# A decoder layer in f32 on one core: GLA score products paired with a later turn, head gates behind the next head's keys and queries, branch outputs stored whole, and another order of the first loads

## The chip, the cores and the metric

The kernel runs on one core of one Trainium2 chip. The metric is device time in microseconds (us) of one execution, taken as the median of several runs.

## The reference

One layer of a hybrid trunk is computed in f32 on 16 meta tokens and 1024 tokens of width 1024. An RMS norm is followed by one wide projection `h @ w_in + b_in`, whose columns are the inputs of four GLA heads, four mLSTM heads and two merge gates. A GLA head is gated linear attention with a decay per channel:

```
diff = bc[t] - bc[s]                       # running sums of log decay, per channel
scores[t, s] = sum_k q[t, k] * k[s, k] * exp(diff[t, s, k])     for s <= t
out = inter + scores @ v
o_gla = head_rms(out) * silu(g_r)
```

The mLSTM heads are a matrix memory behind a short convolution. Both branches are normed per head, multiplied by their head gate, projected, merged as `sigmoid(gate_a) * (o_gla @ w_bg) + sigmoid(gate_b) * (o_ml @ w_bm)`, projected again and added to the input. A convolutional gated MLP and a last norm follow.

## The kernel before, in words

Every large product is made of three: each operand is split into a high part H and a rest L (types that TensorE streams at one pass), and H·H, H·L and L·H are added in PSUM. The split of a loaded weight is `prep` (L96): a DMA on SyncE's queue into one of two `wr` buffers, an ACT copy that makes `wH_...`, a DVE subtraction that makes `wL_...`. The units are loaded in the order in which `head_units` and `gate_units` name them.

The stages are these.

1. Start (L323 to L344). Nine token tiles `xt` (the first holds the 16 meta tokens) are loaded; `norm_x` squares and sums a tile on ACT (`xj`), takes the root on GpSimd (`xr`), scales on DVE, transposes eight blocks on TensorE into PSUM (`xtp`, L316), and splits the result into `xH` (ACT, L318) and `xL` (DVE, L320), which stay in SBUF as the moving operands of all projections.
2. Heads (L861 to L874). `main` walks the projections: `proj_cm` (L146) makes 24 products for each third of the tokens (`TH_ALL`, `TH_POST`: 342 to 348 columns; for head 0 quarters, `SEG_ALL`, `SEG_POST`), `proj_v` (L172) 24 products of 256 columns for each token tile. After each such group `advance` takes one step of the head that was projected before (`gla`, `mlstm`; each `yield` is a step), so that TensorE has a long group between two short steps. Before the change the order for head s is: gate of s (`gate_proj`, the rows `r`), keys and queries of s+1, values of s+1, merge gate a.
3. A GLA head (L551). The scores of each 128 token chunk are built level by level: `level(b)` (L610) scales keys of the early half and queries of the late half of each block of 2b tokens against the block's middle, on DVE (L624, L625, L628), ACT (L626) and GpSimd (L627). For b = 1, 2, 4, 8, 16 `scores_later` (L580) makes one f32 product per chunk, 128 rows by the 64 late columns, and copies what lies in the blocks by a mask into `A` (L589). For b = 32 and 64 `scores_pair` (L567) makes four products of 128 columns, each for two chunks. The diagonal comes first (L564, copied by mask in L565). The running state, the outputs `op` (L720, L721) and their squares follow; `post` (L510) scales each chunk by its norm (L520), transposes it on TensorE (`ot`, L530), multiplies by the gate (L532), splits it into `oH` and the rest (L540, L541) and stores both. `of` and `oH` have one buffer each.
4. Behind head 0 stands `small_rows` (L450), the scalar gates of all four mLSTM heads: two scans and some 1040 element rows on DVE, activations with other tables on ACT.
5. Merge (L917 to L960). `load_o` (L884) loads the H and L parts of eight output tiles for each branch; `bg` and `bm` are the branch products (L909). Then come the output product (L1193), the FFN up (L1107) and the FFN down (L1323), which the change doesn't touch.

The instruction order of each engine comes from a scheduler, which works on the program's order with the priorities that `hp` sets.

Of the kernel before, what the change touches and what calls it, by code (L numbers as in the profile page):

```python
# [1 line left out]

# [6 lines left out]
F32 = mybir.dt.float32  # L9
F32R = mybir.dt.float32r  # L10
U8 = mybir.dt.uint8
# [33 lines left out]
def hybrid_kernel(ctx, tc, x, meta, norm_mix, w_in, b_in, gla_w_gate, gla_b_gate, gla_norm,  # L45
# [60 lines left out]
    lrHL = [wp.tile([P, NK, P], F32R, name=f"w{p}_lr", tag="w" + p) for p in "HL"]  # L106
    for t in lrHL:
        nc.vector.memset(t.bitcast(F32), 0.0)
# [104 lines left out]
    def head_units(s):  # L213
        h = s % 4
        if s < 4:
            uk[s], uq[s] = u_cm(w_in, O_GK + P * h, f"gk{h}"), u_cm(w_in, O_GQ + P * h, f"gq{h}")
            if s == 0:
                uk["lr"] = U.add()
            uv[s] = u_v(O_GV + DV * h, f"gv{h}_")
        else:  # L220
            uk[s], uq[s] = u_cm(w_in, O_MK + P * h, f"mk{h}"), u_cm(w_in, O_MQ + P * h, f"mq{h}")
            uv[s] = u_v(O_MV + DV * h, f"mv{h}_")

    def gate_units(s):
        h = s % 4
        o = (O_GR if s < 4 else O_MO) + DV * h
        ur[s] = [u_cm(w_in, o + P * j, f"r{s}_{j}") for j in range(2)]

    head_units(0)
    for s in range(8):  # L230
        gate_units(s)
# [25 lines left out]
    va = hd.tile([P, T], F32, name="va", tag="oH", bufs=1)[:, :P]  # L257
# [31 lines left out]
    xts = []  # L289

    def load_x(*tiles):
        for i in tiles:
            n = NM if i == 0 else P
            tag, bufs = [("w", 5), ("q", 2), ("k", 2)][(i >= 5) + (i >= 7)]
            xt = hd.tile([P, T], F32, name=f"xt{i}", tag=tag, bufs=bufs)
# [3 lines left out]
    def norm_x(i):  # L299
# [4 lines left out]
        junk = hd.tile([P, T], F32, name=f"xj{i}", tag="of", bufs=1)  # L304
# [7 lines left out]
        for g in range(2):  # L312
            tp = ps.tile([P, 4, P], F32, name=f"xtp{i}_{g}", tag="s", bufs=3)
# [3 lines left out]
            h4 = xH[:, 4 * g:4 * g + 4, c0:c0 + n]  # L317
            nc.scalar.activation(h4, tp[:, :, :n], AF.Copy)  # L318
            l4 = xL[:, 4 * g:4 * g + 4, c0:c0 + n]
            nc.vector.tensor_tensor(l4, tp[:, :, :n], h4.bitcast(F32), OP.subtract)  # L320
# [11 lines left out]
    load_x(4, 5)  # L332
    U.get(2, 0)
    norm_x(3)
    load_x(6, 7, 8)
    for dst, ap in small:
        nc.sync.dma_start(dst, ap)
    for i in range(4, NC + 1):
        if i == NC:
            columns()  # L340
        last = norm_x(i)
    for t, c in ((xH, 0), (xL, 32)):
        m3 = xM[:, :48 * NK].rearrange("p (k w) -> p k w", w=48)
        nc.scalar.activation(m3[:, :, c:c + NM], t[:, :, :NM].bitcast(F32), AF.Copy)  # L344
    floor[0] = tc.cur_priority
# [8 lines left out]

    def cc(i):
        return col[:, i:i + 1]


    with tc.issue_after(last.ins):
        lmask = {}  # L360
        mfs = hd.tile([P, T], F32, name="mfs", tag="raw", bufs=1)
        for i, b in enumerate((16, 8, 4, 2, 1)):
            mf = mfs[:, 64 * i:64 * (i + 1)]
            half = mf.rearrange("p (n w) -> p n w", w=b)
            nc.gpsimd.memset(half, 1.0)
            nb = P // (2 * b)
            nc.gpsimd.affine_select(out=half, in_=half, compare_op=OP.is_ge, fill=0.0, base=0,
                                    pattern=[[-2 * b, nb], [0, b]], channel_multiplier=1)
            nc.gpsimd.affine_select(out=half, in_=half, compare_op=OP.is_ge, fill=0.0, base=b - 1,
                                    pattern=[[2 * b, nb], [0, b]], channel_multiplier=-1)  # L370
            mu = hd.tile([P, 64], U8, name=f"mu{b}")
            nc.vector.tensor_copy(mu, mf)
            lmask[b] = mu
        mu = hd.tile([P, P], U8, name="mu0")
        nc.vector.tensor_copy(mu, ident)
        lmask[0] = mu
        big = hd.tile([P, P], F32, name="big")
# [5 lines left out]
    osc = {(g, p): dram.tile([NK, P, NP], F32, name=f"osc{g}{p}") for g in "gm" for p in "HL"}  # L383
# [5 lines left out]
    def head_proj(s):  # L389
# [7 lines left out]
        if s < 4:  # L397
# [4 lines left out]
            if s == 0:  # L402
                yield from together(pk, pq, proj_cm(uk["lr"], SEG_ALL, 0, lambda p, t0, n: nc.scalar.activation(
                    raw_s[0:96, t0:t0 + n], p[0:96, :], AF.Identity, bias=bsm[0:96])))
# [14 lines left out]
    def gate_proj(s):  # L419
        hh = heads[s]  # L420
        hh["r"] = []
        for j in range(2):
# [3 lines left out]
            yield from proj_cm(ur[s][j], TH_POST, T0, lambda p, t0, n, r=r, c=c: nc.scalar.activation(  # L426
# [83 lines left out]
    def post(s, o, om, sc, ncols, last):  # L510
# [13 lines left out]
        for j in range(2):  # L524
            r = hh["r"][j]
            of = hd.tile([P, T], F32, name=f"of{s}_{j}", tag="of", bufs=1)
# [12 lines left out]
            oH = hd.tile([P, NP], F32R, name=f"oH{s}_{j}", tag="oH", bufs=1)  # L539
            nc.scalar.activation(oH, of[:, :NP], AF.Copy)  # L540
            nc.vector.tensor_tensor(of[:, :NP], of[:, :NP], oH.bitcast(F32), OP.subtract)  # L541
            nc.sync.dma_start(osc[g, "H"][2 * h + j], oH.bitcast(F32))
            nc.sync.dma_start(osc[g, "L"][2 * h + j], of[:, :NP])
# [7 lines left out]
    def gla(s):  # L551
# [7 lines left out]
        def scores(lt, rt, b):  # L559
            for g in range(2):  # L560
                pt = ps.tile([P, 4, P], F32, name=f"sc{s}_{b}_{g}", tag="s", bufs=3)
                for i in range(4):
                    c = 4 * g + i
# [872 lines left out]
```

## Time and profile before

| | us |
|---|---|
| median of 3 runs | 1971.62 (1969.85 to 1973.77) |
| the profiled execution | 1973.3 |
| its span, first to last instruction | 1971.4 |
| TensorE busy, matmuls / weight loads | 1936.3 / 1854.0 |
| DVE / ACT / GpSimd busy | 963.4 / 744.3 / 286.5 |

In the profile PE is TensorE's matmul row, PEld its weight loads, POOL is GpSimd, SP the queue that issues DMAs. A matmul of two f32 operands stands in the trace as two records (320 records in L586 for the 160 products of the program), a product of split operands as one. A matmul's recorded time reaches past the start of the next one, so that slots are read from start to start. PEclk is the clock granted to TensorE, 1.00 being full. An idle time stands at the instruction that ended it, with what released it.

### The profile page before, as it was taken

Reading aid. Unit: us, or ns where it says so; the run is one execution under the profiler, and the core shown is the slowest. Engines: PE = TensorE matmul, PEld = TensorE weight load, DVE = VectorE, ACT = ScalarE, POOL = GpSimd, SP = SyncE. Lnnn points to the kernel's source line nnn. Section 1 sums busy time; section 2 is a strip of 40 time slices with the busy share of each in tenths; the row PEclk is TensorE's granted clock in tenths of the full one; section 3 lists DMA queues with packets and bytes.
Section 4 is the critical chain, followed back from the end, with each engine's and each line's share of the span. In section 5 each row is a group of like instructions: output and inputs, shape, how many; then the busy total and the mean of one; then the engine's idle time right before and its main releaser. Section 6 shows DMA issues by size and latency. Waiting matters only on the chain. (4 is left out here: it accounts for less than half of the span.)

```text
span 1971.4 us, 31346 instructions
## 1 busy us (share of the span) xinstructions
PE 1936.3 (98%) x13333; PEld 1854.0 (94%) x13333; DVE 963.4 (49%) x1427; ACT 744.3 (38%) x1176; POOL 286.5 (15%) x201
## 2 busy tenths in 40 slices
PE   7999999999999999999999999999999999999998
PEld 6999999999999999999999999999999999978886
DVE  6265263637535343422022446698888888710202
ACT  5145333535534343423221234544545444431211
POOL 2020020101000000000000002012222222364220
PEclk9999999999999999999999999999999999999999
DMA  4210403232234222226971433333333333487731
GB/s 152 57 33 23 100 22 95 37 70 69 61 96 90 64 88 63 79 62 123 315 268 54 150 108 108 124 102 126 116 119 123 118 118 113 170 301 263 239 101 43
DMA packets 191271, 224.82 MB, mean 114 GB/s; under 512 B 11102, under 2 KB 150640, under 8 KB 191131
## 3 DMA queue, kind: packets, MB, share of 16 engines
q1 hardware_dynamic: 190843, 221.76, 37.2%
q8 instruction: 105, 1.72, 0.4%
q10 hardware_dynamic: 288, 1.05, 0.1%
q14 instruction: 35, 0.29, 0.0%
HBM read 166.07 MB, written 56.71 MB: 113 GB/s over the span
## 5 line engine op out<-in xcount | busy, mean ns | idle before, releaser
L1323 PE MATMUL pd<-ringH,a 128*128 128x512 f32 x416 | 131.6, 393 | 1.5 <-DMA a<-adrL 1.5
L154 PE MATMUL pj<-xH,wH_r 128*128 128x342 f32 x384 | 124.2, 323 | 0.4 <-ACT r L426 0.4
L154 PE MATMUL pj<-xH,wL_r 128*128 128x342 f32 x384 | 122.9, 320 | 0.0
L154 PE MATMUL pj<-xL,wH_r 128*128 128x342 f32 x384 | 122.5, 319 | 0.0
L1357 DVE TENSOR_TENSOR acc<-pd,acc 128x512 f32<-128x512 f32 x16 | 11.1, 692 | 196.3 <-PE pd L1323 196.3
L1323 PEld LDWEIGHTS pd<-ringH,a 128*128 128x128 f32 x416 | 78.0, 188 | 19.6 <-DMA a<-adrL 2.0
L1323 PE MATMUL pd<-ringL,a 128*128 128x512 f32 x208 | 82.5, 397 | 1.5 <-POOL ringL L1302 1.5
L197 PE MATMUL pv<-wH_gv,xH 128*128 128x256 f32 x256 | 75.4, 294 | 0.0
L197 PE MATMUL pv<-wH_mv,xH 128*128 128x256 f32 x256 | 74.2, 290 | 0.0
L1193 PE MATMUL po<-wL_wo,yH 128*128 128x256 f32 x256 | 72.0, 282 | 2.0 <-DVE wL_wo L103 2.0
L1193 PE MATMUL po<-wH_wo,yH 128*128 128x256 f32 x256 | 72.8, 284 | 0.9 <-DVE h L1200 0.9
L154 PEld LDWEIGHTS pj<-xH,wH_r 128*128 128x128 f32 x384 | 72.2, 188 | 1.1 <-ACT r L426 0.5
L627 POOL TENSOR_TENSOR pk<-pk,kT 128x512 f32<-128x512 f32 x24 | 40.2, 1685 | 226.9 <-ACT pk L626 226.8
L197 PE MATMUL pv<-wL_gv,xH 128*128 128x256 f32 x256 | 72.7, 284 | 0.0
L197 PE MATMUL pv<-wH_gv,xL 128*128 128x256 f32 x256 | 72.6, 283 | 0.0
L154 PEld LDWEIGHTS pj<-xL,wH_r 128*128 128x128 f32 x384 | 72.2, 188 | 0.0
L154 PEld LDWEIGHTS pj<-xH,wL_r 128*128 128x128 f32 x384 | 72.2, 188 | 0.0
L197 PE MATMUL pv<-wL_mv,xH 128*128 128x256 f32 x256 | 71.9, 281 | 0.0
L197 PE MATMUL pv<-wH_mv,xL 128*128 128x256 f32 x256 | 71.9, 281 | 0.0
L1193 PE MATMUL po<-wH_wo,yL 128*128 128x256 f32 x256 | 71.8, 281 | 0.0
L1154 DVE SCALAR_TENSOR_TENSOR cv<-u,fc,cv 128x1024 f32<-128x1024 f32 x44 | 69.4, 1578 | 0.4
L201 DVE TENSOR_TENSOR v<-pv,bB 128x256 f32<-128x256 f32 x64 | 27.0, 421 | 78.1 <-PE pv L197 77.9
(618 smaller groups left out, 6714.5 us busy)
## 6 DMA issues: line engine op xcount, KB each, us to landing
rd<-in_ffn_w_down_dram SPq DMA_DIRECT2D x36, 512.0 KB, 5.9
rg<-in_ffn_w_up_dram SPq DMA_DIRECT2D x22, 512.0 KB, 4.2
ru<-in_ffn_w_up_dram SPq DMA_DIRECT2D x22, 512.0 KB, 3.8
a<-adrH SPq DMA_DIRECT2D x44, 256.0 KB, 5.0
a<-adrL SPq DMA_DIRECT2D x44, 256.0 KB, 4.7
adrH<-aH SPq DMA_DIRECT2D x21, 512.0 KB, 2.6
adrL<-aL SPq DMA_DIRECT2D x21, 512.0 KB, 2.6
wr_r<-in_w_in_dram SPq DMA_DIRECT2D x16, 512.0 KB, 4.0
```

The source lines that it names most:

```text
L154: nc.tensor.matmul(pt[:, :n], a[:, k, :], b[:, k, base + t0:base + t0 + n], start=(i == 0), stop=(i == 3 * NK - 1))
L197: nc.tensor.matmul(pt[:, :DV], a[:, k, t0:t0 + P], b[:, k % 4, :], start=(i == 0), stop=(i == 3 * NK - 1))
L201: nc.vector.tensor_tensor(vt[:n, c, :DV], pt[:n, :DV], bB[:n, :], OP.add)
L627: nc.gpsimd.tensor_tensor(pe, pe, lv(kv, b)[:, :, 0, :], OP.mult)
L1154: nc.vector.scalar_tensor_tensor(y, u[:, j:SEQ + j], fc[:, j, jj:jj + 1], y, OP.mult, OP.add)
L1193: nc.tensor.matmul(pt[:, :DV], a, b[:, k % 4, :], start=(k == 0 and i == 0), stop=(k == NK - 1 and i == len(terms) - 1))
L1323: nc.tensor.matmul(pts[t][n], a[:, c], b[:, 512 * n:512 * n + 512], start=start and i == 0, stop=stop and i == 2)
L1357: nc.vector.tensor_tensor(acc[:, h], pts[t][n], acc[:, h], OP.add)
```

## The change

In the GLA heads the five small levels are laid out as the large ones were: of a pair of chunks the early halves of the even one stand as they are, those of the odd one from back to front, so that four products of 128 columns hold eight chunks (`scores_small`). The odd chunks' scores are then the wrong way round in time, and one f32 product with a matrix of ones on the other diagonal (`flip`), 128x512, turns them (`turn`); ACT copies the result into a tile of its own, `An`. The diagonal and the level b = 32 follow the turn. The early half's subtraction on DVE and multiplication (or copy) on GpSimd become two instructions, one of them writing from back to front.

For heads 0 to 5 the next head's keys and queries stand ahead of this head's gate. Head 0's first gate tile is projected with its keys and queries, in quarters; the small columns `lr` come behind, in thirds. `small_rows` moves from head 0 to head 3. `post` stores one whole f32 tile instead of two parts; `load_o` loads it and splits it on ACT and DVE. `of` has two buffers. At the top stand eight products of the identity with itself, the first token tile's load comes ahead of `gmix`, keys' and queries' weights ahead of the third token tile, and four small rows are issued from ACT's queue.

```diff
-    lrHL = [wp.tile([P, NK, P], F32R, name=f"w{p}_lr", tag="w" + p) for p in "HL"]
+    lr2 = hd.tile([P, 2, NK, P], F32R, name="w_lr", tag="v", bufs=2)
...
+    GATE_LATER = [s < 6 for s in range(8)]
...
     for s in range(8):
+        if GATE_LATER[s]:
+            kq_units(s + 1)
         gate_units(s)
...
-            tp = ps.tile([P, 4, P], F32, name=f"xtp{i}_{g}", tag="s", bufs=3)
+            tp = ps.tile([P, 4, P], F32, name=f"xtp{i}_{g}", tag="pj" if i == 1 else "s", bufs=3)
...
-    load_x(0)
-    nc.sync.dma_start(gmix, rowb(norm_mix, 0, D))
-    load_x(1, 2)
-    norm_x(0)
-    norm_x(1)
-    U.get(0, 0)
-    load_x(3)
-    U.get(1, 0)
-    norm_x(2)
...
+    def idle_products(n, name):
+        pt = ps.tile([P, P], F32, name=f"idle{name}", tag="ot", bufs=2)
+        for _ in range(n):
+            nc.tensor.matmul(pt, ident, ident, start=True, stop=True)
+    idle_products(8, "a")
+    for dst, ap in small[:4]:
+        nc.scalar.dma_start(dst, ap)
+    load_x(0, 1)
+    nc.sync.dma_start(gmix, rowb(norm_mix, 0, D))
+    load_x(2)
+    norm_x(0)
+    norm_x(1)
+    U.get(0, 0)
+    U.get(1, 0)
+    norm_x(2)
+    load_x(3)
...
-                yield from together(pk, pq, proj_cm(uk["lr"], SEG_ALL, 0, lambda p, t0, n: nc.scalar.activation(
+                yield from together(pk, pq, gate_proj(0, (0,)))
+                yield from proj_cm(uk["lr"], TH_ALL, 0, lambda p, t0, n: nc.scalar.activation(
...
-            oH = hd.tile([P, NP], F32R, name=f"oH{s}_{j}", tag="oH", bufs=1)
-            nc.scalar.activation(oH, of[:, :NP], AF.Copy)
-            nc.vector.tensor_tensor(of[:, :NP], of[:, :NP], oH.bitcast(F32), OP.subtract)
-            nc.sync.dma_start(osc[g, "H"][2 * h + j], oH.bitcast(F32))
-            nc.sync.dma_start(osc[g, "L"][2 * h + j], of[:, :NP])
+            nc.sync.dma_start(osc[g][2 * h + j], of[:, :NP])
...
+        An = hd.tile([P, T], F32, name=f"An{s}", tag="of", bufs=2)[:, :512].rearrange("p (i t) -> p i t", t=P)
+        Ac = [An[:, c // 2, :] if c % 2 else A[:, c, :] for c in range(NC)]
...
+        def turn():
+            pt = ps.tile([P, 4, P], F32, name=f"sct{s}", tag="s", bufs=3)
+            nc.tensor.matmul(pt, flip, A.rearrange("p (i c) t -> p i c t", c=2)[:, :, 1, :], start=True, stop=True)
+            nc.scalar.activation(An, pt, AF.Copy)
+        def products(pk, b):
+            pt = ps.tile([P, 4, P], F32, name=f"sc{s}_{b}", tag="s", bufs=3)
+            for i in range(4):
+                nc.tensor.matmul(pt[:, i, :], pk[:, P * i:P * (i + 1)], pk[:, 512 + P * i:512 + P * (i + 1)], start=True, stop=True)
+            return pt
...
-        def scores_later(pk, b):
-            n = P // (2 * b)
-            pt = ps.tile([P, NC, 64], F32, name=f"sc{s}_{b}", tag="s", bufs=3)
-            for c in range(NC):
-                l = lv(pk[:, P * c:P * (c + 1)], b)[:, :, 1, :]
-                nc.tensor.matmul(pt[:, c, :], pk[:, P * c:P * (c + 1)], l, start=True, stop=True)
-            dst = A.rearrange("p c (n h w) -> p c n h w", h=2, w=b)[:, :, :, 1, :]
...
+        def scores_small(pk, b):
+            pt = products(pk, b)
+            dst = A.rearrange("p (i c) (n h w) -> p i (c n) h w", c=2, h=2, w=b)[:, :, :, 1, :]
...
+            if b < 32:
+                e = pk[:, :512].rearrange("p (i n h w) -> p i n h w", n=64 // b, h=2, w=b)
+                pe = [e[:, :, :, 0, :], e[:, :, ::-1, 1, ::-1]]
...
-                nc.vector.tensor_tensor(pe, ref, b4[:, :, 0, :], OP.subtract)
+                for e, _, t in early:
+                    nc.vector.tensor_tensor(e, t[..., b - 1:b].to_broadcast(t.shape), t, OP.subtract)
...
-                nc.gpsimd.tensor_tensor(pe, pe, lv(kv, b)[:, :, 0, :], OP.mult)
+                for e, k, _ in early:
+                    nc.gpsimd.tensor_tensor(e, e, k, OP.mult)
...
             if b == 64:
-                scores_pair(pk, 32)
+                yield
+                turn()
+                yield
+                scores_diagonal()
+                scores_large(pk, 32)
...
-        if s == 0:
+        if s == 3:
             side.append(small_rows())
-        main(gate_proj(s))
-        if s < 7:
-            main(head_proj(s + 1))
+        nxt = head_proj(s + 1) if s < 7 else iter(())
+        if GATE_LATER[s]:
+            main(islice(nxt, 6))
+        main(gate_proj(s, (0, 1) if s else (1,)))
+        main(nxt)
...
-            for p in "HL":
-                nc.sync.dma_start(t[p, k // 4][:, k % 4, :NP].bitcast(F32), osc[g, p][k])
+            h, l = (t[p, k // 4][:, k % 4, :NP] for p in "HL")
+            nc.sync.dma_start(l.bitcast(F32), osc[g][k])
+            nc.scalar.activation(h, l.bitcast(F32), AF.Copy)
+            nc.vector.tensor_tensor(l, l.bitcast(F32), h.bitcast(F32), OP.subtract)
```

What moves on the engines is shown at three places. The first is TensorE's queue in head 0's levels; `sc_b` is the product of level b, `sc_0` the diagonal, `sct` the turn, and between two of these rows stand one or two groups of a projection. Before:

```order
L564 MATMUL sc_0_0_1021<-qT_415,kT_414 128x128 x4
L564 MATMUL sc_0_1_1027<-qT_415,kT_414 128x128 x4
...
L586 MATMUL sc_1_1171<-pk_1_1102 128x64 x8
...
L586 MATMUL sc_2_1213<-pk_2_1165 128x64 x8
...
L586 MATMUL sc_4_1265<-pk_4_1207 128x64 x8
...
L572 MATMUL sc_32_1397<-pk_32_1343 128x128 x4
```

The same place after the change:

```order
L616 MATMUL sc_1_1238<-pk_1_1167 128x128 x4
...
L616 MATMUL sc_2_1278<-pk_2_1230 128x128 x4
...
L616 MATMUL sc_4_1318<-pk_4_1270 128x128 x4
...
L609 MATMUL sct_1475<-A,flip 128x512
...
L602 MATMUL sc_0_0_1504<-qT_431,kT_430 128x128 x4
L602 MATMUL sc_0_1_1510<-qT_431,kT_430 128x128 x4
L616 MATMUL sc_32_1516<-pk_32_1397 128x128 x4
```

Each small level is four products of 128 columns where it was eight of 64, the turn is one product of 512 columns, and the diagonal stands behind it, directly ahead of level 32.

The second place is the top of SyncE's queue, which issues the loads (`wr_gk`, `wr_gq`: weights of head 0's keys and queries; `xt`: token tiles). Before:

```order
L296 DMA xt_107<-in_meta_dram 16x1024
L324 DMA gmix<-in_norm_mix_dram 128x1024
L296 DMA xt_110<-in_x_dram 128x1024
L296 DMA xt_112<-in_x_dram 128x1024
L99 DMA wr_gk_158<-in_w_in_dram 128x8x128
L296 DMA xt_164<-in_x_dram 128x1024
L99 DMA wr_gq_166<-in_w_in_dram 128x8x128
```

After:

```order
L313 DMA xt_119<-in_meta_dram 16x1024
L313 DMA xt_121<-in_x_dram 128x1024
L359 DMA gmix<-in_norm_mix_dram 128x1024
L313 DMA xt_124<-in_x_dram 128x1024
L100 DMA wr_gk_170<-in_w_in_dram 128x8x128
L100 DMA wr_gq_176<-in_w_in_dram 128x8x128
L313 DMA xt_204<-in_x_dram 128x1024
```

The first full token tile has moved ahead of `gmix`, and the queries' weights ahead of the third full tile. Five small rows, the fourth tile and the gate's weights follow.

The third place is DVE's queue where `small_rows` (the rows `sr`) meets the norm of the head in front of it (`rs..v` goes to GpSimd, which returns `rs..r`). Before, behind head 0:

```order
L90 TENSOR_SCALAR rs0v<-ss_1543 128x9
L464 SCALAR_TENSOR_TENSOR sr_1957<-rmask,sr_1957 4x1040
L201 TENSOR_TENSOR v_1501<-pv_5_1710,bB_1223 128x256
L520 TENSOR_SCALAR or_0_1576<-or_0_1576,rs0r 128x256 x4
```

After, behind head 3:

```order
L497 SCALAR_TENSOR_TENSOR sr_4944<-raw_s,sr_4943 4x1040
L91 TENSOR_SCALAR rs3v<-ss_4519 128x9
L499 SCALAR_TENSOR_TENSOR sr_4943<-sr_4944,raw_s 4x1040
L558 TENSOR_SCALAR or_0_4552<-or_0_4552,rs3r 128x256 x4
```

One scan stands between the norm's input and the scaling in both; the meeting has moved from head 0 to head 3, and with it from the value groups of a projection to a merge gate's.

More of the change, by code (lines that the diff above doesn't have):

```diff
@@ L1 @@
 from contextlib import ExitStack
+from itertools import islice
 import concourse.bass as bass
@@ L361, in hybrid_kernel @@
         mfs = hd.tile([P, T], F32, name="mfs", tag="raw", bufs=1)
[L362 to L373, printed above, removed]
+        nc.gpsimd.memset(mfs[:, :P * 6], 1.0)
+        for sg in (1, -1):
+            nc.gpsimd.affine_select(out=mfs[:, :P], in_=mfs[:, :P], compare_op=OP.is_ge, fill=0.0, base=-sg * (P - 1),
+                                    pattern=[[sg, P]], channel_multiplier=sg)
+        flip = hd.tile([P, P], F32, name="flip")
+        nc.vector.tensor_copy(flip, mfs[:, :P])
         mu = hd.tile([P, P], U8, name="mu0")
```

151 lines of the change are left out of this document (90 added, 61 removed).

## The prediction

> **What bounds the kernel now.** I read the page's busy times first, then the busy time by stages, then the list of what TensorE waited for.
>
> ```profile
> span 1971.4 us, 31346 instructions
> ...
> PE 1936.3 (98%) x13333; PEld 1854.0 (94%) x13333; DVE 963.4 (49%) x1427; ACT 744.3 (38%) x1176; POOL 286.5 (15%) x201
> ```
>
> TensorE is busy for 98% of the span and its weight loads for 94%; no other engine passes 49%. The span is the sum of TensorE's slots and its few idle stretches, so an edit is worth what it takes from these two. The stages say where the idle time lies (the first number is the length, the second TensorE's busy time):
>
> ```profile
> 0.00:25.00 25.00, 11.82 (x57) 10.28 (x58) 19.31 (x47) 16.58 (x33) 7.43 (x15) 0.87 0.77 240
> ...
> 150.00:200.00 50.00, 48.45 (x325) 45.18 (x324) 27.67 (x46) 24.91 (x42) 4.60 (x3) 0.97 0.14 42
> 200.00:400.00 200.00, 198.69 (x1385) 191.36 (x1384) 95.34 (x141) 78.91 (x130) 22.81 (x16) 1.00 0.26 58
> 400.00:600.00 200.00, 199.53 (x1318) 191.16 (x1317) 96.30 (x156) 90.14 (x160) 15.63 (x16) 1.00 0.30 74
> ...
> 900.00:950.00 50.00, 50.00 (x322) 49.58 (x321) 9.90 (x12) 13.43 (x19) 0.00 (x0) 1.00 0.85 188
> ```
>
> In the first 25 us 13.2 are idle. In the heads it is 1.6 + 1.3 + 0.5 = 3.3 us, at the merge nothing. The waits name the heads' part:
>
> ```profile
> PE ot L530 <- DVE or L520: 1.6, 1, 1.6
> ...
> PE sc L564 <- DVE of L532: 0.6, 2, 0.5
> PE otm L537 <- DVE of L538: 0.6, 1, 0.6
> ...
> PE pj L154 <- ACT r L426: 0.4, 1, 0.4
> ```
>
> The sum is made against the profiled execution, 1973.3 us (1.9 of them outside the span). The median of the runs, 1971.62, is 1.7 less, and I take these off at the end.
>
> **The change part by part.** *The small products.* One level of head 0, and level 32, which already has the new shape, each with the next group's first product behind it:
>
> ```profile
> 110.16 1.90 PE L586 MATMUL sc<-pk 128*128 128x64 f32 x16
> 111.87 0.40 PE L154 MATMUL pj<-xH,wH_r 128*128 128x342 f32 x1
> ...
> 138.11 1.05 PE L572 MATMUL sc<-pk 128*128 128x128 f32 x8
> 138.92 0.40 PE L154 MATMUL pj<-xH,wH_gq 128*128 128x342 f32 x1
> ```
>
> From start to start a level of eight 64 column products holds TensorE for 1.71 us, four products of 128 columns for 0.81. A record costs 0.107 or 0.101 us: half the columns are no cheaper, the number of products counts.
>
> ```profile
> L586 PE MATMUL sc<-pk 128*128 128x64 f32 x320 | 37.9, 271 | 0.0
> ```
>
> 320 records are 20 levels, so 20 x (1.71 - 0.81) = 18.0 us go; if the new records took the old ones' 0.107, 20 x (1.71 - 0.86) = 17.0. I take 18.0.
>
> The Trainium skill, page "TensorE: Matmul & The Clock Gate", section "Back-to-back issue gap", gives a warm matmul N / 2.4 + 2.5 ns; estimated from that, 320 records of 64 columns (29 ns) and 160 of 128 (56 ns) come to 9.3 and 9.0 us, and this part to 0.3 instead of 18.0. The trace has 107 ns at 64 columns and disagrees.
>
> *The turn.* No product of 512 f32 columns stands in the trace; the nearest has 256:
>
> ```profile
> 156.81 0.59 PE L720 MATMUL op<-v,A 128*128 128x256 f32 x2
> 157.24 0.59 PE L721 MATMUL op<-S,qh 128*128 128x256 f32 x2
> ```
>
> Two records take 0.43 us, 0.215 each, twice those of 128 columns. Doubling again gives 0.86 us for a turn and 3.4 for four heads; 1.7 if it cost no more than 256 columns. I take +3.4, the continuation of the doubling.
>
> *What the levels and the turn add elsewhere.* The halves on DVE and GpSimd are two instructions where one was. What covers them:
>
> ```profile
> 110.78 3.71 POOL L627 TENSOR_TENSOR pk<-pk,kT 128x512 f32<-128x512 f32 x2 [50.93 <-ACT pk L626]
> ...
> 115.75 1.00 PE L586 MATMUL sc<-pk 128*128 128x64 f32 x8
> ...
> L310 POOL TENSOR_TENSOR xr<-xv,mhalf 16x1 f32<-16x1 f32 x1 | 0.5, 544 | 3.7 <-DVE ss L696 3.7
> ```
>
> GpSimd has made the factors of levels 2 and 4 by 114.5, half of it, 1.9 us, for level 2 by 112.6, and TensorE takes level 2 at 115.75: 3.1 us to spare. A second instruction adds at most what the smallest one costs, 0.54, and the shorter product in front takes 0.9 of the cover; 1.6 us stay. I put 0. If a reversed write is slow on GpSimd, the excess over that lands on TensorE level by level (rival C). The turn has a copy of 512 columns on ACT behind it, then the diagonal's copy by mask on DVE; by the order one value group stands between the turn and the diagonal, and nothing else queues there: 0. The wider masks are twenty selections on GpSimd instead of ten, while TensorE projects head 0: 0.
>
> *The start.* What it costs now:
>
> ```profile
> 0.00:12.00 12.00, 1.31 (x10) 1.20 (x11) 7.12 (x26) 6.11 (x11) 3.44 (x10) 1.00 0.82 268
> ...
> 15.00:19.00 4.00, 1.80 (x10) 1.14 (x10) 4.00 (x7) 4.00 (x8) 0.55 (x1) 0.91 0.83 194
> 19.00:26.00 7.00, 6.93 (x35) 6.94 (x36) 6.30 (x14) 3.73 (x9) 3.07 (x4) 0.56 0.41 152
> ...
> 19.83 0.57 PE L154 MATMUL pj<-xL,wH_gk 128*128 128x272 f32 x1
> ...
> 36.96 0.39 PE L154 MATMUL pj<-xH,wH_gk 128*128 128x256 f32 x1 [0.39 <-ACT kT L398]
> 37.19 0.28 PE L154 MATMUL pj<-xL,wH_gk 128*128 128x256 f32 x1
> ...
> 37.90 0.27 PE L154 MATMUL pj<-xL,wH_gk 128*128 128x256 f32 x1
> ```
>
> Dense work begins at 19.83, at a granted clock of 0.56 until 26, and the second quarter of the keys at 36.96, when all tiles are transposed. What fills the time is DVE and ACT:
>
> ```profile
> L320 DVE TENSOR_TENSOR xL<-xtp,xH 128x512 fp32r<-128x512 f32 x16 | 10.6, 686 | 2.0 <-ACT xH L318 1.8
> L311 DVE SCALAR_TENSOR_TENSOR xt<-xt,xr,gmix 128x1024 f32<-128x1024 f32 x8 | 10.2, 1284 | 1.2 <-POOL xr L310 1.2
> L318 ACT ACTIVATE xH<-xtp 128x512 fp32r<-128x512 f32 x16 | 9.2, 597 | 8.0 <-PE xtp L316 7.9
> ...
> L103 DVE TENSOR_TENSOR wL_gq<-wr_gq,wH_gq 128x1024 fp32r<-128x1024 f32 x1 | 1.2, 1216 | 0.0
> ...
> L102 ACT ACTIVATE wH_gq<-wr_gq 128x1024 fp32r<-128x1024 f32 x1 | 1.1, 1058 | 0.0
> ```
>
> New order: the queries' weights are the sixth load, 2.7 MB in all, at 268 GB/s landed by about 10.5 us. ACT then makes `wH_gq` (1.1) and the first tiles' `xH` (four of 0.6 and two small), so the first products start near 14.5, 5.3 us sooner. But DVE still owes six tiles at 1.28 + 2 x 0.69, the first two tiles' rests and two weight rests (1.2 each): 16 + 2.7 + 2.4 = 21 us from about 15, so the last tile ends near 36 as before. What is won is what TensorE does beside that: by the order 25 products of the second quarters stand ahead of the last tile's transposes, which once stood ahead of all. At (37.90 - 37.19) / 6 = 0.118 us these are 3.0 us. Between 2 (the clock at half until 26) and 4.5 (full from 18). I take -3.0. The eight idle products, 16 records at about twice 0.107 on a cold clock, last some 3.4 us in a stretch of 12 us in which TensorE has 1.3 us of work, so they delay nothing; the clock fell from 0.91 to 0.56 behind the gaps of 15 to 19, so what they raise won't last to 14 either: 0, both ways. The gate tile in quarters and `lr` in thirds exchange 96 short products for 72 long ones, one against the other: 0. The four rows on ACT's queue stand ahead of a first tile that isn't there yet: 0.
>
> *Gates behind keys and queries, `small_rows` behind head 3, two `of` buffers.* The groups are the same. The waits on `of` and `r` (0.6 + 0.6 + 0.4) came where transposes stood in a burst; now 24 products part them: -1.6. The wait on `or`:
>
> ```profile
> 179.40 2.32 DVE L464 TENSOR_TENSOR_SCAN sr<-rmask,sr 4x1040 f32<-4x1040 f32 x1
> 179.51 3.81 POOL L92 TENSOR_TENSOR rs0r<-rs0v,mhalf 128x9 f32<-128x9 f32 x1 [5.58 <-DVE rs0v L90]
> ...
> 185.50:189.00 3.50, 3.50 (x19) 3.50 (x19) 3.37 (x7) 1.06 (x1) 0.00 (x0) 0.51 0.02 5
> ```
>
> The root on GpSimd ran beside a scan of `small_rows` and took 3.81 us; TensorE idled 1.6, and the clock fell to 0.51 for 3.5 us, 1.7 more. The meeting moves to head 3, where the cover is three gate groups instead of three value groups, of 342 columns against 256, estimated at 0.118 x 342 / 256 = 0.158 a record: 3 x 24 x (0.158 - 0.118) = 2.9 us more cover. That should swallow 1.6, but the activations of `small_rows` still sit before the norm on ACT. I take -2.4 of the 3.3, so -4.0 for this part, between 0 and -4.9.
>
> The Trainium skill, same page, section "Why this matters for your kernels", asks for no idle gaps over about 3 us to keep the clock. Here 1.6 us of idle time went ahead of half clock, so the row is harsher, and the new waits below are priced by the row; by the page each would cost 1.7 us less.
>
> *Whole outputs.*
>
> ```profile
> 969.24 0.88 SPq L893 DMA_DIRECT2D ogL<-oscgL  x1
> ...
> 976.54 0.32 PE L909 MATMUL bg<-ogH,wH_bg 128*128 128x342 f32 x1
> ...
> L540 ACT ACTIVATE oH<-of 128x1026 fp32r<-128x1026 f32 x16 | 17.0, 1062 | 47.7 <-DVE of L538 43.6 <-issue 4.0
> ...
> L541 DVE TENSOR_TENSOR of<-of,oH 128x1026 f32<-128x1026 f32 x16 | 19.6, 1227 | 16.3 <-ACT oH L540 16.2
> ```
>
> The last of sixteen loads is issued 7 us before the first use; eight are left. The split moves from the heads to the merge, 8.5 us of ACT and 9.8 of DVE a branch, where 50 us have 13.4 and 9.9 busy. On ACT it stands ahead of the gates' copies out of PSUM, which have three buffers: 0; uncovered it would cost its first tile, 2.3.
>
> Sum: -18.0 + 3.4 - 3.0 - 4.0 = -21.6. 1973.3 - 21.6 = 1951.7, less 1.7: **1950.0**.
>
> **The rivals.** *B: the small parts are eaten.* The start gives nothing, as DVE ends at the same time anyway, and two of the four heads wait at the turn, whose diagonal, copies and last small level now stand close together, 1.6 + 1.7 each with the clock: 1950.0 + 3.0 + 6.6 = 1959.6. For it: value groups are short. Against: the order has scaled keys and factors ahead there.
>
> *C: slower.* GpSimd's reversed writes set the pace. From product to product a small level would have 24 x 0.158 + 0.81 = 4.6 us. In 16 levels (2 to 16, four heads) the halves would have to take 4.6 + 21.6 / 16 = 6.0 us to eat the gain, against 1.9 for a whole now. At 7 us it is 16 x 2.4 - 21.6, slower by 17: 1988. For it: no reversed write is in the trace. Against: it needs three times the time.
>
> *D: the columns count.* If a slot followed columns, 4 x 128 would take what 8 x 64 does, 1.71, and the first term is 0: 1968.0, within 0.2%. The page's formula above says this; the row of 0.81 speaks against it.
>
> **How the numbers follow.** This kernel's measurement can tell about 0.2%, 3.9 us, from no change. My forecast has 0.82, B 0.10, C 0.04, D 0.04. Faster: A and B, 0.92; same: D, 0.04; slower: C, 0.04. The range: at best 18.0 with 1.7 for the turn, 4.5 and 4.9, a gain of 25.7, 1945.9; at worst of A 17.0, 3.4, 2.0 and 0, a gain of 15.6, 1956.0; it reaches to B, and 2 us lower for the stages behind, whose waits may shift: 1944 to 1961.
>
> **What would show it.** The small levels as 160 records of 128 columns, 0.81 a level; `sct` at 0.86 from start to start; second quarter of the keys near 34; no waits of TensorE on `of`, and little on `or`. Wrong would be waits of `sc` on GpSimd (C), of `k0t` or `sc` on ACT at the turn (B), or levels still at 1.7 (D).

## The result and the profile after

The changed kernel takes 1959.55 us (median of 4 runs, 1958.12 to 1960.79), the kernel before 1971.43 beside it: a ratio of 0.9936, 95% interval 0.9923 to 0.9949. It is faster by 11.9 us where the working had 21.6; the time lies inside the range, close to what rival B gave, though not for B's reasons. A second measurement (below) gave 0.9927 [0.9915, 0.9940].

The head of the page of the changed kernel, to be held against that of before:

```profile
span 1958.9 us, 31082 instructions
...
PE 1927.9 (98%) x13197; PEld 1842.2 (94%) x13197; DVE 967.6 (49%) x1443; ACT 750.5 (38%) x1183; POOL 304.3 (16%) x229
```

The span is 12.5 us shorter. TensorE has 136 records less (160 small products fewer, 8 for the turns and 16 idle ones more) and the same busy share. The small levels and the turn look as they were costed. From the timeline of TensorE in head 0, start and duration first:

```profile
112.58 1.05 PE L616 MATMUL sc<-pk 128*128 128x128 f32 x8
113.39 0.40 PE L155 MATMUL pj<-xH,wH_gq 128*128 128x342 f32 x1
...
117.94 1.16 PE L616 MATMUL sc<-pk 128*128 128x128 f32 x8 [0.51 <-POOL pk L679]
...
138.65 1.02 PE L609 MATMUL sct<-A,flip 128*128 128x512 f32 x2
139.11 0.68 PE L198 MATMUL pv<-wH_gv,xH 128*128 128x256 f32 x1
139.63 0.27 PE L198 MATMUL pv<-wL_gv,xH 128*128 128x256 f32 x1
```

A level holds TensorE for 113.39 - 112.58 = 0.81 us. The turn's two records end late: the product behind them starts 0.46 later but holds TensorE for 0.52 instead of 0.12, so that the turn takes 139.63 - 138.65 - 0.12 = 0.86 us. Both are the predicted numbers, and rival D (the columns count) is out. The Trainium skill, page "TensorE: Matmul & The Clock Gate", section "Back-to-back issue gap", has 128 columns at 56 ns by its formula for a lone product, and says that this is too little in a stream, where 81 ns were measured. Here eight records of 128 columns take 0.81 us, 101 ns each.

Three landmarks show how far the changed kernel is ahead. The first value product, before and after:

```profile
62.62 0.28 PE L184 MATMUL pv<-wH_gv,xM 128*128 128x256 f32 x1
...
976.54 0.32 PE L909 MATMUL bg<-ogH,wH_bg 128*128 128x342 f32 x1
```

```profile
70.60 0.28 PE L185 MATMUL pv<-wH_gv,xM 128*128 128x256 f32 x1
...
959.08 0.32 PE L968 MATMUL bg<-ogH,wH_bg 128*128 128x342 f32 x1
```

In front of the value product there is now a gate tile, 96 records of about 0.119, 11.4 us: 70.60 - 11.4 = 59.2 against 62.62, so the start has won 3.4. At the first branch product (second row of each) the lead is 17.46, and it stays so to 0.1 us through both branches and the output product: the split of the loaded outputs costs nothing. At the end of TensorE's last product it is 12.7. Put against the terms:

| part | predicted | these two profiles |
|---|---|---|
| small levels, 20 of them | -18.0 | -18.0 |
| turn, four heads | +3.4 | +3.4 |
| start | -3.0 | -3.4 |
| waits and clock in the heads | -4.0 | +0.5 (the rest to -17.5) |
| FFN, not touched | 0 | +4.7 |

Two terms failed. What TensorE waited for, of the heads and of the FFN, in the changed kernel:

```profile
PE sct L609 <- DVE A L633: 2.4, 2, 2.3
...
PE pd L1382 <- DMA a<-adrL: 2.1, 1, 2.1
...
PE X L1166 <- ACT u2raw L1195: 1.7, 1, 1.7
...
PE ot L568 <- DVE or L558: 1.0, 2, 0.8
...
PE sc L616 <- POOL pk L679: 0.5, 1, 0.5
```

The old waits of the heads on `of`, `r` and the scaled outputs behind head 0 are gone, as said. In their place stands 2.3 us ahead of one turn, 0.8 ahead of transposes, and 0.5 ahead of level 2. In the FFN the waits on `u2raw` (0.5 before) and `adrL` (1.5 before) are longer.

The +0.5 is what is left over between two landmarks. Read directly, between the first value product and the first branch product TensorE is idle for 4.1 us where it was for 3.3, and the 1.7 us that a lowered clock took behind head 0 are gone, which makes -1.0. Some 1.5 us between the two readings are not accounted for.

### The profile page after: what moved, and what is told of

Read it like the earlier page. It is cut to its first block, busy times and chain, and to the rows that moved or that the text cites. A ratio compares the mean times of both kernels' runs of the same rounds, so it can differ in the third digit from the quotient of the medians.

```text
span 1958.9 us, 31082 instructions
## 1 busy us (share of the span) xinstructions
PE 1927.9 (98%) x13197; PEld 1842.2 (94%) x13197; DVE 967.6 (49%) x1443; ACT 750.5 (38%) x1183; POOL 304.3 (16%) x229
## 5 line engine op out<-in xcount | busy, mean ns | idle before, releaser
L155 PE MATMUL pj<-xH,wH_r 128*128 128x342 f32 (+2 forms) x392 | 126.6, 323 | 0.0
L155 PE MATMUL pj<-xH,wL_r 128*128 128x342 f32 (+2 forms) x392 | 124.3, 317 | 0.0
L155 PE MATMUL pj<-xL,wH_r 128*128 128x342 f32 (+2 forms) x392 | 124.1, 317 | 0.0
L679 POOL TENSOR_TENSOR pk<-pk,kT 128x256 f32<-128x256 f32 (+1 forms) x40 | 56.3, 1437 | 185.6 <-ACT pk L677 104.1
```

What stands on the lines that cost most here:

```text
L155: nc.tensor.matmul(pt[:, :n], a[:, k, :], b[:, k, base + t0:base + t0 + n], start=(i == 0), stop=(i == 3 * NK - 1))
L679: nc.gpsimd.tensor_tensor(e, e, k, OP.mult)
```

## The experiments

The theory after these two profiles: levels, turn and start are worth their terms, and the moves around them exchange old waits for new ones. The rivals: the turn's wait is made by the scalar rows, or by the gates' new place; the idle products carry the start; the FFN's loss is the change's own. What the runs gave, each beside the kernel before on the same chip (its medians there were 1973.28, 1972.09 and 1972.37):

| kernel | us | ratio to before |
|---|---|---|
| no idle products | 1957.68 | 0.9929 [0.9916, 0.9943] |
| pairs alone | 1977.70 | 1.0026 [1.0014, 1.0038] |
| rows behind head 0 | 1972.08 | 0.9993 [0.9984, 1.0002] |
| gate of head 3 first | 1955.69 | 0.9911 [0.9898, 0.9925] |
| all gates first | 1955.26 | 0.9911 [0.9898, 0.9925] |
| pairs and rows | 1960.02 | 0.9934 [0.9922, 0.9947] |
| rows alone | 1973.71 | 1.0009 [1.0000, 1.0018] |
| before again | 1972.17 | 1.0001 [0.9992, 1.0010] |
| empty steps | 1980.90 | 1.0041 [1.0028, 1.0053] |
| gates first, no idle products | 1955.04 | 0.9913 [0.9900, 0.9926] |
| the same, DRAM padded | 1954.06 | 0.9905 [0.9892, 0.9918] |
| changed kernel again | 1956.94 | 0.9927 [0.9915, 0.9940] |

**The pairs by themselves.** The kernel before with the new masks and the new `gla`; since it has one buffer of each output tile, the turned scores lie in that of `oH`:

```diff
-        An = hd.tile([P, T], F32, name=f"An{s}", tag="of", bufs=2)[:, :512].rearrange(...)
+        An = hd.tile([P, NP], F32R, name=f"An{s}", tag="oH", bufs=1)[:, :512].bitcast(F32).rearrange(...)
```

> The kernel before with the paired levels and the turn alone (start, order of the gates, scalar rows behind head 0 and split stores as before). Theory one (the terms of the levels stand by themselves): -17.5 for the levels and +3.6 for four turns, 13.9 less than before, 1957.5; then start, gates and stores together have cost 2 us in the changed kernel. Theory two (the turn waits when the gates stand in front): one or more turns wait for the copy by mask, 2 to 3 us each, and the half clock of 1.7 behind head 0 stays: 1959 to 1963.

It was slower than before by 4.4 us: both theories missed. Between the first value product and the first branch product TensorE is idle for 15.8 us where before it was for 3.3. A lowered clock takes another 6.8 where it took 1.7 (summed over windows of 5 us, each with its length times what the granted clock lacks of 1.00). Without these two the stretch is 15.0 us shorter, so the 14.6 us that levels and turn save are there, and 17.6 us of waiting and clock stand against them. Of its waits in the heads:

```profile
PE sct L581 <- DVE A L605: 5.2, 3, 2.0
PE ot L536 <- DVE or L526: 3.4, 2, 1.8
PE ot L536 <- DVE of L538: 3.1, 5, 1.1
PE pj L154 <- ACT r L432: 2.6, 3, 1.2
```

Three turns wait, then the transposes and the gates' copies. All but the last are on DVE. In the stretch of head 1's levels DVE has no gap, and TensorE is idle for 2.5 us (length, then busy time of TensorE, its loads, DVE, ACT and GpSimd, and the granted clock):

```profile
240.00:268.00 28.00, 25.50 (x197) 24.74 (x196) 28.00 (x42) 10.57 (x13) 12.24 (x10) 1.00 0.15 39
```

**The scalar rows behind head 0, the rest as changed.**

```diff
-        if s == 3:
+        if s == 0:
             side.append(small_rows())
```

> The changed kernel with the scalar rows behind head 0 again. Theory one (the move is worth what the old stall cost): the wait of the transposes on the scaled outputs behind head 0 comes back, 1.6 us idle and up to 1.7 at half clock, 1961 to 1963; the turn of head 3 still waits 2.3 us. Rival one (the gates in front cover it wherever it stands): 1959.5. Rival two (the rows cause the wait at head 3's turn): that wait goes, 1957.

By the ratios 11 to 13 us of the gain were gone, by none of the waits that I had expected. From the first value product to the first branch product TensorE is idle for 12.9 us instead of 4.1, and a lowered clock, which took nothing there in the changed kernel, takes 5.1. The waits of TensorE in this kernel's heads:

```profile
PE sc L616 <- DVE pk L680: 9.9, 6, 3.3
PE sc L616 <- POOL pk L679: 2.0, 3, 1.2
```

It is the small levels of heads 1 to 3, far from the rows, that wait. Where they lie is seen in the timeline; a level of head 1 in the changed kernel:

```profile
234.84 0.32 PE L155 MATMUL pj<-xH,wL_r 128*128 128x342 f32 x1
235.00 1.05 PE L616 MATMUL sc<-pk 128*128 128x128 f32 x8
```

The third level of head 1 with the rows behind head 0:

```profile
255.90 0.28 PE L198 MATMUL pv<-wH_gv,xL 128*128 128x256 f32 x1
256.56 1.16 PE L616 MATMUL sc<-pk 128*128 128x128 f32 x8 [0.38 <-POOL pk L679]
```

Each group of a projection is followed by one step of the head behind it, and `small_rows` has seven steps. In front of head 1's they push its levels seven groups later, from gate, key and query groups (24 x 0.157 = 3.8 us) behind value groups (24 x 0.118 = 2.8 us). From one level to the next a pair has then 3.6 us of TensorE's time instead of 4.6, and DVE's part of a level no longer fits. Busy time in the stretch of head 1's levels, in the columns named above; first before the change:

```profile
245.00:278.00 33.00, 33.00 (x270) 33.00 (x269) 28.76 (x39) 13.41 (x22) 10.57 (x6) 1.00 0.12 33
```

In the changed kernel:

```profile
216.00:243.00 27.00, 27.00 (x185) 27.00 (x184) 25.83 (x35) 13.45 (x18) 11.95 (x10) 1.00 0.09 22
```

With the rows behind head 0:

```profile
241.00:267.00 26.00, 23.17 (x194) 22.58 (x193) 25.82 (x37) 10.40 (x14) 10.43 (x9) 1.00 0.08 21
```

DVE was busy for 87% of that stretch before, and is for 96% in the changed kernel, where TensorE still has no gap; at 99% it sets the pace and TensorE is idle for 2.8 of 26 us. GpSimd, on which rival C stood, is busy for under half of it.

**Empty steps.** The sharpest test of this: no instruction is added and the rows stay behind head 3, but where their steps stood, ahead of head 1's, stand steps that do nothing.

```diff
+        if s == 0:
+            side.append(iter(range(7)))
         if s == 3:
             side.append(small_rows())
```

> The changed kernel with seven empty steps put between the steps of head 0 and those of head 1; no instruction is added, the scalar rows stay behind head 3. Theory one (DVE sets the pace: it is busy for 96% of the stretch of head 1's levels in the changed kernel, where they lie behind groups of 342 columns, and for 99% where they lie behind value groups): the levels of heads 1 to 3 move back behind value groups and wait for DVE, 9 to 12 us in sum, about 0.998 to 1.000 of before, as with the rows behind head 0. Rival (the rows' own scans and activations behind head 0 did the damage): as the changed kernel, 0.994.

1980.9 us: 8.5 slower than before and 24 slower than the changed kernel beside it. Two rows of its waits:

```profile
PE sc L616 <- DVE pk L680: 13.4, 8, 3.3
...
PE pj L155 <- ACT r L464: 3.4, 1, 3.4
```

Seven empty steps do all the harm and more, since the steps behind head 3 slip too (the wait on `r`). Between the same two products TensorE is idle for 17.9 us instead of 4.1, and a lowered clock takes 10.2: of the 24 us some 14 are waits and 10 the clock behind them. The rows' scans are not the cause; the place of the levels is.

DVE's busy share alone doesn't tell this. In the stretch of head 1's levels it is 92%, less than the 96% at which the changed kernel has no gap, and TensorE is idle for 5.0 of 27 us:

```profile
243.00:270.00 27.00, 22.04 (x174) 21.51 (x173) 24.87 (x36) 8.38 (x11) 9.47 (x10) 0.94 0.08 20
```

What counts as well is when DVE's part of a level is due. The first level of head 1 waits for it here:

```profile
247.35 0.67 DVE L680 TENSOR_TENSOR pk<-pk,qT 128x512 f32<-128x512 f32 x1
248.17 1.19 PE L616 MATMUL sc<-pk 128*128 128x128 f32 x4 [3.25 <-DVE pk L680]
```

**Rows alone, and pairs with rows.** The same one-line move (`s == 0` to `s == 3`) in the kernel before, and in the kernel with the pairs alone.

> The kernel before with nothing changed but the scalar rows, behind head 3 instead of head 0. Theory one: the 1.6 us of idle time and 1.7 us at half clock behind head 0 go and nothing else does, since the old small levels of 1.71 us wait for nothing wherever they lie: 2 to 3.3 us less, 0.9985. Rival (the meeting only moves): the same wait stands behind head 3, 1.000.

> The kernel with the pairs and the turn alone, and with the scalar rows moved from head 0 to head 3 as well; gate order, start and stores as before, one buffer each for the outputs. Theory one: the rows' steps no longer push the levels of heads 1 to 3 behind value groups, so the waits of the turn (5.2 us) go and those of the transposes on the scaled outputs with them (3.4), and behind head 0 no half clock: some 10 to 14 us less than pairs alone, about 1964 or 0.995 to 0.998 of before. Rival (the pairs need two output buffers or the later gate to be worth anything): waits on of and r stay or grow, 1.000 of before or more.

By themselves the rows gain nothing, 1.0009: the meeting with the root only moves, and it has grown. The wait behind head 3, and TensorE's clock there:

```profile
PE ot L530 <- DVE or L520: 3.1, 1, 3.1
```

```profile
518.00:522.00 4.00, 3.88 (x19) 3.61 (x18) 3.94 (x11) 0.53 (x1) 0.00 (x0) 0.50 0.00 0
```

With the pairs the same move turns 1.0026 into 0.9934, some 18 us, though the wait of 3.1 is there too; the waits at turns, on `of` and on `r` are gone. TensorE's idle time between the first value product and the first branch product falls from 15.8 to 3.4 us, and what a lowered clock takes from 6.8 to 1.7. So +1.6 for the rows and +4.4 for the pairs make -12 together. The expectation had 1964; it had counted one stretch of half clock and left out the others, and the waits on `of` and `r`. 0.9934 is, within the intervals, what the whole change has. At the first branch product the changed kernel is 3.0 us ahead of this one (959.08 against 962.09), which is the start's gain; gates, buffers and whole outputs add nothing to it, and the FFN takes it back (below).

**The gates.** Head 3's gate first again, then all gates first:

```diff
-    GATE_LATER = [s < 6 for s in range(8)]
+    GATE_LATER = [s < 6 and s != 3 for s in range(8)]
```

> The changed kernel with head 3's gate ahead of head 4's keys and queries, as before the change; all other heads as changed. Theory one: head 3's turn waits 2.3 us because the convolution of head 4's queries (three products of 1.3 us on DVE) stands ahead of the mask copy that the turn needs, and it stands there since head 4's queries are projected early; with the gate first the wait goes and the time is 2.3 less, 1957.2. Rival: DVE is full there anyway (scaled keys and queries), the wait stays or moves to another product: 1959.5 within 1.

```diff
-    GATE_LATER = [s < 6 for s in range(8)]
+    GATE_LATER = [False for s in range(8)]
```

> The changed kernel with every head's gate ahead of the next head's keys and queries, as before; the scalar rows stay behind head 3, pairs, turn, two of buffers and start as changed. Theory one (what matters is that the five small levels of a head lie behind groups of 342 columns and not behind value groups; the rows decide that, the order of gate and keys doesn't): all small levels stand behind gate, key or query groups, no wait of a small level on DVE, and the time is the changed kernel's or up to 2.4 us less, since head 3's turn no longer waits: 0.9911 to 0.9936 of before. Rival (the gate's place carries the gain): small levels or transposes wait 6 us or more in sum, 0.997 of before or worse.

Both came out at 0.9911 where 2.4 us, 0.0012, had been expected from 0.9936; against the second measurement, 0.9927, they are 0.0016 better. The intervals overlap, so that the size rests on the trace. The mechanism is seen on DVE's timeline. The changed kernel ahead of head 3's turn:

```profile
460.64 1.22 DVE L718 TENSOR_TENSOR qh<-qh,qT 128x1024 f32<-128x1024 f32 x1
461.77 2.64 DVE L803 SCALAR_TENSOR_TENSOR qc<-qT,col,qc 128x1040 f32<-128x1040 f32 x2
464.33 0.68 DVE L633 COPY_PREDICATED A<-mu,sc 128x512 f32<-128x512 uint8 x1
```

With head 3's gate first:

```profile
459.54 1.21 DVE L718 TENSOR_TENSOR qh<-qh,qT 128x1024 f32<-128x1024 f32 x1
460.67 0.73 DVE L633 COPY_PREDICATED A<-mu,sc 128x512 f32<-128x512 uint8 x1
```

The last mask copy stood behind two convolution products (`qc`, L803) of head 4, whose queries were there early, and the turn started at 465.06. With the gate ahead the copy comes first, the turn starts at 461.60 and waits for nothing. All gates first gives no more than that. In a later head the transposes then wait 1.7 us for their scaled outputs, where they waited 0.8 with the later gates; between the first value product and the first branch product the two kernels take the same, 885.7 and 885.9 us. So the later gates have won nothing on balance, and cost this wait at the turn. The levels of all heads then lie behind key and query groups and wait for 0.3 us in all.

**The idle products.**

```diff
-    idle_products(8, "a")
```

> The eight idle products at the top are taken out, the rest is the changed kernel. What I predicted (they do nothing): the second quarter of the keys starts at the same time, the granted clock stays at 1.00 from 6 to 40 us, and the time is the changed kernel's, 1959.5 within 1. Rival (they keep the clock up): the clock falls to about 0.55 for some 7 us behind the first transposes, as it did in the kernel before between 19 and 26 us, which costs 7 x 0.45 = 3.1 us: 1962.6.

Without them the granted clock in the stretch that had 0.56 before:

```profile
19.00:26.00 7.00, 7.00 (x60) 7.00 (x59) 5.77 (x11) 5.23 (x12) 1.62 (x3) 1.00 0.66 217
```

and the time is no worse, 0.9929 against 0.9936 and 0.9927. The four other profiles with the old start have 1.00 there too, so the 0.56 was that one execution's. Nor does a row at 1.00 mean full speed so early. In the changed kernel, at a granted clock of 1.00:

```profile
20.04 0.43 PE L155 MATMUL pj<-xH,wH_gk 128*128 128x272 f32 x1
...
20.62 0.29 PE L155 MATMUL pj<-xH,wH_gk 128*128 128x272 f32 x1
```

Without the idle products the same change comes between 19.1 and 19.3, and in all nine profiles with the new start between 18.6 and 21.4, with idle products or without. The new order of the loads does the start; the products do nothing for it. The two edits undone together, all gates first and no idle products:

> The changed kernel with every gate ahead of the next head's keys and queries and without the idle products: the two edits that won or lost nothing are undone together. Theory: 2.4 us less than the changed kernel for head 3's turn, nothing for the idle products, 0.9905 to 0.992 of before. Rival (without idle products the clock falls at the start): 3 us more than with them, 0.9925.

0.9913, the same as with the gates alone: again nothing from the idle products.

**The FFN's 4.7 us.** The kernel before and the changed one once more, word for word, and the last kernel with the DRAM tensors of the outputs as long as before:

```diff
-    osc = {g: dram.tile([NK, P, NP], F32, name=f"osc{g}") for g in "gm"}
+    osc = {g: dram.tile([2 * NK, P, NP], F32, name=f"osc{g}") for g in "gm"}
```

> The kernel before once more, word for word, for its stretch from the first branch product to the end: that took 988.1 us in the profile shown and 989.5 to 992.8 in the five other profiles, whose code there is the changed or the unchanged one. Theory one (the length of the waits on u2raw and on the second product's input differs from execution to execution, with half clock behind the longer ones): 989 to 993 here too, so that some 3 us of the difference between the two profiles are not the change's. Rival (the changed kernel's own): 988 again.

> The changed kernel once more, word for word, for the stretch from the first branch product to the end, 992.8 us in its profile against 988.1 and 988.0 in two of the kernel before. Theory one (execution to execution): some 990 here. Rival (the change's own): 992 or more again, with over 1.7 us of waiting on u2raw. The time against before: 0.9936 within 0.0015 by both.

> The same as the kernel with both edits undone, and the stored outputs' tensors in DRAM twice as long, as before the change, half of it unused, so that whatever lies behind them stands where it stood. Theory one (the load of u2raw lands later in the changed kernels because addresses in DRAM have moved): TensorE's wait on it falls from about 1.8 to 0.6 us, the stretch from the first branch product to the end to 988, 2 to 3 us less in all. Rival (it differs from execution to execution): no difference beyond 1 us.

From the first branch product to the end of the last product the kernel before took 988.0 us again (988.1 in the first profile), the changed one 989.7 instead of 992.8, and the ten other profiles lie from 988.2 to 992.9. The unpadded kernel's wait on `u2raw`, with its addresses moved, is as short as the padded one's (0.6 and 0.5), so moved addresses alone don't make that wait longer.

TensorE's idle time and the clock account for nearly all of it: without these two the stretch takes 976.1 to 977.0 us in every one of the fourteen profiles. The first profile of the changed kernel has 1.7 us more idle time than the kernel before, and loses 3.4 us to the clock at two places. The first place: in the 14 us behind the second wait of the FFN's first products it is at 1.00 in the kernel before, both times, and with the pairs and rows, and below in the other eleven, the pairs alone and the rows alone among them. Before, and in the changed kernel:

```profile
1283.00:1297.00 14.00, 11.79 (x99) 11.59 (x98) 13.56 (x20) 5.11 (x7) 0.00 (x0) 1.00 0.32 90
```

```profile
1267.00:1281.00 14.00, 11.79 (x86) 11.59 (x85) 12.77 (x18) 5.21 (x7) 0.00 (x0) 0.88 0.25 74
```

0.12 x 14 = 1.7 us. The second place lies behind the wait on `adrL`, and costs another 1.7. Before, and in the changed kernel:

```profile
1747.00:1749.00 2.00, 2.00 (x10) 1.64 (x9) 0.00 (x0) 0.73 (x1) 0.00 (x0) 1.00 1.04 400
```

```profile
1732.00:1734.00 2.00, 2.00 (x6) 1.52 (x6) 0.00 (x0) 0.02 (x1) 0.00 (x0) 0.51 1.04 399
```

The changed kernel's other profile has the first drop and not the second. The kernel before didn't vary (988 twice), so that theory one of its expectation missed; the changed one did, by 3 us. The nine profiles with the new start average 991.0 and the five with the old one 988.8: some 2.3 of the 4.7 us go with the changed kernels, most of it clock (2.0), and the rest was this execution's. The lowered clock at the first place stands in all nine of the first and in two of the five others. Whether the change brings it on or chance does, these runs can't settle. One thing is unexplained: the wait on `u2raw` is 1.4 to 2.3 us in all six profiles with idle products, and 0.4 to 1.1 in all eight without. What sixteen records at the top have to do with it 1250 us later no run shows.

## Why the prediction was right or wrong

In the two profiles the change won 12.7 us up to the last product where the sum had 21.6. Of the 8.9 us between them 4.5 lie in the waits and the clock of the heads and 4.7 in the FFN, less 0.4 that the start won more.

*Levels and turn* were right to 0.1 us: 0.81 and 0.86. Taking the price of a 64 column record and that of a 512 column product from neighbouring rows of the trace held, where columns alone would have misled.

*Their cover* was put at 0, "the halves on DVE and GpSimd are two instructions where one was", and this is the step whose reasoning failed, although the changed kernel shows only 0.5 us there. I worked the cover out for GpSimd, at one level of head 0, whose levels lie behind long groups in both kernels. The engine that decides is DVE, and the place is heads 1 to 3. The row of that stretch was in the profile of before: 28.76 busy of 33.00. The pairs take 5 x 0.9 = 4.5 us out of it on TensorE's side and nothing on DVE's: 28.5 us for 28.8 of work. From that row it followed that the pairs leave DVE no slack there if nothing else moves. It gives only 0.3 us of loss a head; that pairs alone lost all of their gain, at turns, transposes and in the clock behind them, only the run showed.

*The scalar rows' move* was costed as a matter of one collision, -2.4. Alone it is worth nothing, +1.6; its worth beside the pairs, 11 to 18 us, is that head 1 to 3's levels get longer groups, and this the prediction didn't see at all. In the changed kernel the two mistakes cancel: the cover is there because the rows moved. That the time fell inside the range is in this part luck.

*Waits in the heads*, -4.0, came to +0.5 by the landmarks and to -1.0 by idle time and clock; and the 1.7 us of clock in the -4.0 were that one execution's, since the second profile of the kernel before doesn't have them. The old ones went as said, the wait behind head 0 moved under longer groups and shrank to 0.2 behind head 3. Rival B's mechanism took 2.3 us of the gain, in one head and not in two, and with no lowered clock behind it: the turn waits for DVE because the gates' later place, which I had put at nothing, lets head 4's convolution in ahead of a mask copy. I had looked at what queues behind the turn and not at what stands ahead of its mask copy.

*The start* was right, and for the reasons given: 3.4 in these profiles; nine profiles with the new start against five with the old one have the first value product at 70.2 - 11.4 = 58.8 against 61.9, 3.1 earlier. The second quarter of the keys came at about 30, not 34; the last tile's end hardly moved, as said.

*Whole outputs, idle products, the quartered gate tile*: 0, as said.

*The stages behind* were given 2 us of the range and nothing in the sum. They took 4.7 in these profiles: the sum stood on an execution with no lowered clock there, which only two others of the fourteen share, and one page doesn't show how often that is so.

Rivals C (GpSimd's reversed writes) and D (the columns) are out: the halves cost 1.36 us each, 2.7 for a level that took 1.7, and only level 2 of head 0 waits 0.5 for it. The row:

```profile
L679 POOL TENSOR_TENSOR pk<-pk,kT 128x256 f32<-128x256 f32 x32 | 42.5, 1359 | 176.0 <-ACT pk L677 94.6 <-issue 80.8 <-POOL pk L679 0.6
```

## What to carry to other kernels

When the bounding engine gets a shorter step, take the busy share of every other engine in the stretch where that step lies, and in each of its repeats, not on average: DVE at 49% of the span was at 87% there, and 4.5 us less of TensorE made it the bound. The share tells where to look and not what is lost: TensorE had no gap beside a DVE at 96%, and idled 5.0 of 27 us beside one at 92% whose work came later. In a schedule that pairs a step of one thing with a group of another, seven steps inserted anywhere move everything behind them to other partners; two edits that gain nothing alone (+4.4, +1.6) may gain 12 together, so edits of such a schedule are costed together and tried together. The best kernel of these runs keeps pairs, turn, rows and start, and puts the gates first again without idle products: 0.9913 and, padded, 0.9905 of before, 2 to 4 us less than the change beside them (0.9927), with intervals that overlap.

## What the runs showed of the hardware

The length of an idle stretch did not decide whether the clock fell. Behind head 0 of the kernel before, TensorE waited 1.6 us and was granted 0.51 for 3.5 us in the first profile; in the second, of the same code with a wait of 1.5, the same stretch reads:

```profile
185.50:189.00 3.50, 3.50 (x27) 3.32 (x27) 3.37 (x5) 2.12 (x2) 0.00 (x0) 1.00 0.02 5
```

At the changed kernel's turn of head 3 it waited 2.3 and stayed at 1.00:

```profile
464.00:466.00 2.00, 0.94 (x3) 0.49 (x3) 2.00 (x3) 0.00 (x0) 0.00 (x0) 1.00 0.00 0
466.00:468.00 2.00, 2.00 (x18) 1.97 (x17) 0.22 (x1) 1.75 (x3) 0.10 (x1) 1.00 0.04 8
```

The Trainium skill, page "TensorE: Matmul & The Clock Gate", section "Why this matters for your kernels", allows gaps of up to about 3 us; the turn agrees with it, the first profile does not. So the 1.7 us for the clock behind a wait is a price that an execution pays or doesn't.
